# 256-column products of a two-layer hybrid backbone: high and low operand part side by side under one weight load

## The chip, the cores and the metric

The kernel runs on one core of a Trainium2 chip. The metric is device time in microseconds (us) for one execution; the median of 3 runs of the kernel before is 2346.48 us (2346.24 to 2348.11). TensorE is called PE below, its weight loads PEld, VectorE DVE, ScalarE ACT, GpSimd POOL and SyncE SP.

## The reference

Two layers run over 256 context tokens and 256 latent tokens of 1024 channels. Both layers read all 512 tokens, but the last layer needs only the 256 latent tokens as output, so most of its products have 256 token columns.

```python
def hybrid_mixer(h_lat, h_ctx, p, rope_gqa, rope_diff, lam_init, need_ctx):
    ... = jnp.split(h_lat @ p['w_in'], IN_OFFSETS, axis=-1)
    ... = jnp.split(h_ctx @ p['w_in'], IN_OFFSETS, axis=-1)
    ...                       # state-space scan, grouped-query and differential attention
    y_lat = merge_branches(ssm_l, gqa_l, diff_l, gate_l, p)
    if not need_ctx:
        return y_lat, None

def merge_branches(y_ssm, y_gqa, y_diff, gate_logits, p):
    ...
    m = (g[:, :, 0] * (y_ssm @ p['w_ssm_out'])
         + g[:, :, 1] * (y_gqa @ p['w_gqa_out'])
         + g[:, :, 2] * (y_diff @ p['w_diff_out']))
    return m @ p['w_o']

def swiglu(h, w_in, w_out):
    a, b = jnp.split(h @ w_in, 2, axis=-1)
    return (jax.nn.silu(a) * b) @ w_out
```

Every layer then normalises `alpha * x + gate * sublayer(...)` over the channels (layer norm), once after the mixing and once after the feed-forward.

## The kernel before, in words

Activations lie with channels on the 128 partitions and tokens along the free dimension; 1024 channels are `KT` = 8 blocks. A product block is 128 output channels by 512 tokens (layer 0) or 256 tokens (layer 1, `T0` = 256, `TN` = 256), summed over 8 channel blocks in one PSUM tile (`psd`, at most 6 at a time).

To keep float32 accuracy at the rate of the one-pass type float32r, every operand is split into a high part (a rounded copy, made by ACT) and a low part (the difference, made by DVE; `split`, `load_w`). Each product is three matmuls per channel block: high weight times high activation, high weight times low activation, low weight times high activation. `dense` does this for a whole block, `mm3` for one term. In `dense` a pass over the blocks with the high weight comes first, two matmuls each, and then a pass with the low weight. Each matmul has a weight load of its own.

The stages are: layer-0 mixing (projections `proj`, the state-space steps, both attentions, the gated merge), the output product with `w_o` and a layer norm, layer-0 feed-forward, and the same three for layer 1. The 256-column products in layer 0 are the attention's probability-times-value products (`pv_mm`), `w_o`, and the last piece of the feed-forward's output (each done per half of the tokens). In layer 1 nearly all are: 60 projections, 32 branch outputs, `w_o`, 44 feed-forward input blocks and all feed-forward output blocks. Results are read out of PSUM by whoever needs them next: `sigmoid`, the convolution, the rotation, or the residual step `resid`, which adds the gated product to the residual in one DVE instruction.

Nothing is ordered by hand. A class `Plan` records all instructions and then makes a list schedule: it estimates each one's duration (`cost`), keeps track of on-chip tiles (`SIZES`), and fixes the order on every engine; each engine then runs its list in that order, waiting by semaphores. A tile class `s2` has 65 slots of 128 by 512 words that nearly everything shares; in `s2` a slot can hold two tiles of 256 columns. In the trace a tile in such a shared slot is called `shared`, a whole one `s`, a weight tile `w`, a PSUM tile `ps`. All recorded instructions have the line of the one call that emits them, L586 before and L589 after, so the trace is read by tile names and shapes.

## Time and profile before

| what | us |
|---|---|
| median of 3 runs | 2346.48 |
| span of the profiled execution, first to last instruction | 2345.3 |
| PE busy, of the span | 2301.0 (98%) |
| DVE busy | 1670.1 (71%) |
| ACT busy | 1422.4 (61%) |
| layer-0 mixing, 0 to 1007 | 1007 |
| layer-0 output product and norm, 1007 to 1056 | 49 |
| layer-0 feed-forward, 1056 to 1451 | 395 |
| layer-1 mixing, 1451 to 2098 | 647 |
| layer-1 output product and norm, 2098 to 2135 | 37 |
| layer-1 feed-forward, 2135 to 2326 | 191 |
| last layer norm and output, 2326 to the end | 19.3 |

Only one execution was profiled. Its time outside the span isn't listed; the median of the runs lies 1.2 us above the span. The stage borders are read from the order of the weights in the trace, to a microsecond or so. A busy PE is one whose matmuls overlap without a gap, which says nothing of how far apart they start; for that, a stretch's length is divided by its number of matmuls.

### The profile page before, as it was taken

The page shows a single profiled execution, that of the slowest core. Times are in us where ns is not written, and L with a number is a line of the kernel's source. Part 1 is how long each engine was busy: PE and PEld are TensorE (multiplying, and loading weights), DVE is VectorE, ACT ScalarE, POOL GpSimd, SP SyncE. Part 2 cuts the span into 40 slices and gives each one's busy share as a digit, 9 for nine tenths or more (in the row PEclk, how much of TensorE's full clock was granted, in tenths as well). Part 3 has the DMA queues.
Part 4 walks back from the last instruction along what each step waited for, and adds up shares of the span by engine and source line. Part 5 has one row for each costly group of instructions (what it writes and reads, how often), then busy time and mean ns, then how long its engine had stood idle before and what let it go on. Part 6 is the DMA issues. An engine that isn't in the chain of part 4 may idle for free. (4 is left out here: it accounts for less than half of the span.)

```text
span 2345.3 us, 38903 instructions
## 1 busy us (share of the span) xinstructions
PE 2301.0 (98%) x14423; PEld 1940.3 (83%) x14423; DVE 1670.1 (71%) x3438; ACT 1422.4 (61%) x2887; POOL 135.1 (6%) x216
## 2 busy tenths in 40 slices
PE   8999999999999999999999999999999999999998
PEld 4877777887887788898777778989988798998997
DVE  3889857888988864476333337999698888767655
ACT  4778745867767753345323235888586676646554
POOL 3102102000100100000000000001010100000000
PEclk9999999999999999999999999999999999999998
DMA  9746544332433465576555425527443345798662
GB/s 332 214 135 175 181 132 135 102 112 72 133 104 98 133 216 175 184 219 213 171 163 168 139 74 151 150 76 217 132 129 114 105 126 164 214 274 240 191 188 66
DMA packets 520702, 370.37 MB, mean 158 GB/s; under 512 B 20706, under 2 KB 472674, under 8 KB 520512
## 3 DMA queue, kind: packets, MB, share of 16 engines
q1 hardware_dynamic: 507296, 329.63, 47.3%
q0 software_dynamic: 13216, 38.25, 5.5%
q8 instruction: 113, 1.85, 0.3%
q14 instruction: 77, 0.63, 0.1%
HBM read 334.00 MB, written 33.82 MB: 157 GB/s over the span
## 5 line engine op out<-in xcount | busy, mean ns | idle before, releaser
L586 PE MATMUL ps<-s,w 128*128 128x512 f32 (+2 forms) x7608 | 1524.0, 355 | 8.2 <-DVE s L586 4.6
L586 PEld LDWEIGHTS ps<-s,w 128*128 128x128 f32 (+1 forms) x7608 | 1236.0, 189 | 237.1 <-issue 28.8
L586 ACT CAST w<-w 128x1024 fp32r<-128x1024 f32 (+2 forms) x486 | 454.4, 944 | 486.3 <-DVE w L586 256.8
L586 DVE TENSOR_TENSOR w<-w,w 128x1024 fp32r<-128x1024 f32 (+2 forms) x486 | 528.0, 1092 | 299.8 <-PE ps L586 203.0
L586 PE MATMUL ps<-shared,w 128*128 128x256 f32 x2544 | 313.2, 283 | 0.0
L586 PE MATMUL ps<-s,s 128*64 128x128 f32 (+6 forms) x2320 | 303.2, 361 | 7.6 <-DVE s L586 2.1
L586 PEld LDWEIGHTS ps<-shared,w 128*128 128x128 f32 x2544 | 308.5, 192 | 0.5 <-issue 0.3
L586 ACT ACTIVATE s<-s 128x512 f32<-128x512 f32 x424 | 260.6, 630 | 31.0 <-DVE s L586 24.7
L586 PEld LDWEIGHTS ps<-s,s 128*64 128x64 f32 (+3 forms) x2320 | 186.9, 152 | 90.6 <-issue 31.9
L586 DVE TENSOR_TENSOR s<-s,s 128x512 f32<-128x512 f32 (+2 forms) x298 | 196.2, 674 | 36.7 <-ACT s L586 34.5
L586 DVE TENSOR_TENSOR s<-s,ps 128x512 f32<-128x512 f32 x116 | 79.1, 684 | 133.3 <-PE ps L586 65.7
L586 DVE SCALAR_TENSOR_TENSOR s<-ps,misc,s 128x510 f32<-128x510 f32 (+2 forms) x188 | 139.3, 741 | 13.9 <-ACT s L586 11.8
L586 PE MATMUL ps<-w,s 128*128 128x256 f32 x960 | 119.7, 284 | 0.0
L586 PEld LDWEIGHTS ps<-w,s 128*128 128x128 f32 x960 | 117.2, 192 | 2.2 <-issue 1.5
L586 DVE TENSOR_TENSOR shared<-shared,shared 128x256 f32<-128x256 f32 (+2 forms) x241 | 97.2, 417 | 24.4 <-ACT shared L586 22.6
L586 DVE TENSOR_TENSOR s<-ps,s 128x256 fp32r<-128x256 f32 (+1 forms) x204 | 85.6, 444 | 30.4 <-ACT s L586 25.7
L586 ACT ACTIVATE shared<-shared 128x256 f32<-128x256 f32 x232 | 92.4, 416 | 23.4 <-DVE shared L586 20.7
L586 ACT CAST s<-ps 128x256 fp32r<-128x256 f32 (+1 forms) x204 | 74.4, 396 | 36.0 <-PE ps L586 32.1
L586 ACT ACTIVATE s<-ps,misc 128x512 f32<-128x512 f32 x68 | 50.6, 744 | 73.2 <-PE ps L586 73.0
L586 POOL DMA_DIRECT2D s<-dram x96 | 71.9, 753 | 375.0 <-PE ps L586 274.7
L586 ACT ACTIVATE s<-ps,tiny 128x512 f32<-128x512 f32 x112 | 76.7, 689 | 26.5 <-DVE tiny L586 18.9
L586 DVE SCALAR_TENSOR_TENSOR shared<-ps,misc,shared 128x256 f32<-128x256 f32 (+2 forms) x144 | 67.2, 478 | 29.4 <-PE ps L586 20.4
(102 smaller groups left out, 1512.5 us busy)
## 6 DMA issues: line engine op xcount, KB each, us to landing
w<-in_w_in_dram SPq DMA_DIRECT2D x200, 512.0 KB, 4.0
s<-in_ada_w_dram SPq DMA_DIRECT2D x192, 256.0 KB, 4.9
w<-in_ffn_w_in_dram SPq DMA_DIRECT2D x88, 512.0 KB, 3.9
s<-dram POOLq DMA_DIRECT2D x96, 256.0 KB, 5.6
s<-dram SPq DMA_DIRECT2D x64, 256.0 KB, 4.1
w<-in_w_ssm_out_dram SPq DMA_DIRECT2D x32, 512.0 KB, 4.1
w<-in_ffn_w_out_dram SPq DMA_DIRECT2D x32, 512.0 KB, 3.9
shared<-dram SPq DMA_DIRECT2D x112, 128.0 KB, 3.9
```

What stands on the lines that cost most here:

```text
L586: getattr(attr[op.eng], fn)(*[real(v) for v in args], **{a: real(v) for a, v in kw.items()})
```

## The change

For an operand of 256 columns, high and low part are now kept beside each other in one tile of 128 x 2 x 256 (`operand`; for the layer's input streams a new tile class `x4`, 8 tiles of 128 x 2 x 512, `stream`). `side_by_side` then does one matmul of 512 columns with the high weight, which fills a whole PSUM bank (high product in columns 0 to 255, low product in 256 to 511), and one of 256 columns with the low weight, added to the first half. So there are two matmuls for each term where there were three; the columns that stream through are as many as before.

The two halves of the bank must be added. `summed` does it by an ACT copy of the second half into a new tile and a DVE addition of the first half; what read PSUM before now reads that tile. For the residual steps, `resid_halves` does `resid` twice, once for each half. In the attentions, the transposed probabilities of both query halves now go into one PSUM tile per 256 keys (`to_keys`), so the transposes wait for both.

By the loops in the code, 1712 terms are changed: 96 in layer-0 attention, 128 in layer-0 `w_o`, 96 in the last piece of layer-0 feed-forward output, 800 in layer-1 mixing (480 in 60 projections, 256 in 32 branch outputs, 64 in attention), 64 in layer-1 `w_o`, 528 in layer-1 feed-forward (352 in, 176 out). 184 products get `summed` (32 in layer-0 attention, 108 in layer-1 mixing, 44 in layer-1 feed-forward); 24 grouped-query outputs lose an ACT copy that they had before. 64 residual steps become two (16 and 8 after `w_o`, 16 and 24 in the feed-forward).

Three things come with it. `s2` has 49 slots instead of 65, since `x4` takes the room of 16. The planner's cost of a float32r matmul is changed to columns / 2.4 plus weight columns / 9.6 ns. And `HALVES`, the number of first projections of a layer that are done in two halves of 256 columns the old way, now counts only projections over all 512 tokens, so three projections of layer 1 that were done with 512-column matmuls are done in halves: 72 matmuls more. As the planner orders everything anew, hardly a row of any engine stays where it was.

```diff
-SIZES = {"cst": 1, "id": 1, "w4": 15, "s2": 65, "misc": 4, "tiny": 40, "ps": 8}
+SIZES = {"cst": 1, "id": 1, "w4": 15, "x4": 8, "s2": 49, "misc": 4, "tiny": 40, "ps": 8}
...
             if rhs.dt() == F32R:
-                return max(n / 2.4 if n >= 256 else 4 * n / 2.4, 107) + 2.5
+                return (n if n >= 256 else 4 * n) / 2.4 + m / 9.6
...
+    def operand(n):
+
+        if n == 256:
+            t = plan.tile("s2", [128, 2, 256], F32R)
+            return t[:, 0, :], t[:, 1, :], t
+        return t2(n, F32R), t2(n, F32R), None
+
+    def side_by_side(ps, terms):
+
+        both = ps.rearrange("p (a b) -> p a b", b=256)
+        for k, (wh, _, x) in enumerate(terms):
+            T.matmul(both, wh, x[2], start=k == 0, stop=False)
+        for k, (_, wl, x) in enumerate(terms):
+            T.matmul(ps[:, 0:256], wl, x[0], start=False, stop=k == len(terms) - 1)
+
+    def summed(ps):
+        s = t1()
+        A.copy(s, ps[:, 256:512])
+        V.tensor_tensor(s, s, ps[:, 0:256], ALU.add)
+        return s
...
+    def product(w, kn, xs, n):
+        if n == 256:
+            return summed(halves_of(w, kn, xs))
+        ps = psd()
+        dense(ps[:, 0:n], w, kn, xs)
+        return ps
...
+    def stream(x0):
+
+        t = plan.tile("x4", [128, 2, NT], F32R)
+        return t[:, 0, x0:], t[:, 1, x0:], t[:, :, NT - 256:]
...
             w = load_w(W[:, col:col + cols], KT, cols, step)
+            if a:
+                return product(w, KT, xcols(a, NT), NT - a)
             ps = psd()
             half[0] -= 1
-            if half[0] >= 0 and a == 0:
+            if half[0] >= 0:
...
+        def resid_halves(o, d, ps, prev, gm, r):
+            resid(o, d, ps[:, 256:512], prev, gm, r)
+            resid(o, d, ps[:, 0:256], o, gm, r)
...
-                ps = psd()
-                dense(ps[:, 0:256], w, KT, lambda k: tuple(a[:, t0 - T0:t0 - T0 + 256] for a in mm[k]))
-                resid(rt[d, t0], d, ps[:, 0:256], xa, 2, r)
+                resid_halves(rt[d, t0], d, halves_of(w, KT, lambda k: mm[k][t0]), xa, 2, r)
...
+                if not need_ctx:
+                    pab.append(product(w, KT, lambda k: hT[k], TN))
+                    continue
...
-            passes = [[s] for s in segs] if j1 == 22 else [segs]
+            passes = [[s] for s in segs] if j1 == 22 or not need_ctx else [segs]
```

On PE, in the last piece of layer 1's feed-forward output: `ps_24723` is the sum of the second channel block in the order before, `shared_...` its activation tiles (high and low of one block share a tile, hence x2), `w_4687` its high weight and `w_4688` its low weight.

```order
L586 MATMUL ps_24723<-shared_28_24647,w_4687_24565 128x256 x2
L586 MATMUL ps_24723<-shared_3_24717,w_4687_24565 128x256 x2
L586 MATMUL ps_24723<-shared_28_24361,w_4688_24598 128x256
L586 MATMUL ps_24723<-shared_39_24438,w_4688_24598 128x256
L586 MATMUL ps_24723<-shared_30_24505,w_4688_24598 128x256
```

The same place of the change, `ps_23598` being the sum of the fourth channel block:

```order
L589 MATMUL ps_23598<-s_4719_23494,w_4745_23501 128x512
L589 MATMUL ps_23598<-s_4731_23567,w_4745_23501 128x512
L589 MATMUL ps_23598<-s_4671_23260,w_4746_23526 128x256
L589 MATMUL ps_23598<-s_4683_23318,w_4746_23526 128x256
L589 MATMUL ps_23598<-s_4695_23377,w_4746_23526 128x256
```

Where two matmuls of 256 columns stood for the high weight, one of 512 stands now; those for the low weight are as they were.

On DVE, at the end of layer-1 mixing, the branch outputs before: `ps` tiles are products, the `w` rows make low weights of 128 x 1024.

```order
L586 TENSOR_TENSOR shared_56_21458<-shared_56_21458,ps_21931 128x256
L586 TENSOR_TENSOR shared_56_21458<-shared_56_21458 128x256
L586 TENSOR_TENSOR shared_46_20488<-shared_56_21458,shared_36_19583 128x256
L586 TENSOR_TENSOR shared_25_21358<-shared_25_21358,ps_21964 128x256
L586 TENSOR_TENSOR w_4221_22008<-w_4219_21819,w_4220_21968 128x1024
```

And in the change:

```order
L589 TENSOR_TENSOR shared_53_20701<-shared_53_20701,ps_21231 128x256
L589 TENSOR_TENSOR shared_36_20542<-shared_36_20542,shared_53_20701 128x256
L589 TENSOR_TENSOR shared_36_20542<-shared_36_20542 128x256
L589 TENSOR_TENSOR w_4265_21283<-w_4263_21176,w_4264_21269 128x1024
L589 TENSOR_TENSOR s_4222_21280<-shared_36_20542,s_4222_21280 128x256
```

The row that multiplied the gate straight with the PSUM tile has become two: one adds the halves, the next multiplies the sum.

On DVE at the program's end, the last two channel blocks' residual steps before, each followed by the addition that collects the layer norm's sum (`shared_16_21337`), and the first step of the norm itself (it reads `ps_24883`):

```order
L586 SCALAR_TENSOR_TENSOR shared_50_22480<-ps_24839,misc_12157,shared_50_22480 128x256
L586 TENSOR_TENSOR shared_16_21337<-shared_16_21337,shared_50_22480 128x256
L586 SCALAR_TENSOR_TENSOR shared_50_22480<-ps_24860,misc_12157,shared_50_22480 128x256
L586 TENSOR_TENSOR shared_16_21337<-shared_16_21337,shared_50_22480 128x256
L586 SCALAR_TENSOR_TENSOR shared_49_23274<-ps_24883,shared_49_23274 128x256
```

And in the change:

```order
L589 SCALAR_TENSOR_TENSOR shared_53_20701<-ps_23650,misc_11982,shared_53_20701 128x256 x2
L589 TENSOR_TENSOR shared_67_22361<-shared_67_22361,shared_53_20701 128x256
L589 SCALAR_TENSOR_TENSOR shared_38_22415<-ps_23666,misc_11982,shared_38_22415 128x256 x2
L589 TENSOR_TENSOR shared_67_22361<-shared_67_22361,shared_38_22415 128x256
L589 SCALAR_TENSOR_TENSOR shared_16_10462<-ps_23685,shared_16_10462 128x256
```

The residual step stands twice (x2) in front of each addition.

## Rows read from the trace of the kernel before

**Rows 1.** The page's first part: span, then busy us (share) xinstructions by engine

```profile
span 2345.3 us, 38903 instructions
PE 2301.0 (98%) x14423; PEld 1940.3 (83%) x14423; DVE 1670.1 (71%) x3438; ACT 1422.4 (61%) x2887; POOL 135.1 (6%) x216
```

**Rows 2.** Windows by stage: start:end length, busy us (xinstructions) by engine, granted clock, DMA

```profile
core 0: us, PE busy (x) PEld busy (x) DVE busy (x) ACT busy (x) POOL busy (x), PEclk, DMA share, GB/s
0.00:1007.00 1007.00, 988.66 (x5504) 782.33 (x5505) 745.63 (x1677) 647.68 (x1387) 92.90 (x151) 0.99 0.52 156
1451.00:2098.00 647.00, 637.73 (x4595) 572.61 (x4594) 549.60 (x1158) 475.98 (x1034) 42.22 (x65) 0.99 0.54 156
2098.00:2135.00 37.00, 31.73 (x246) 25.86 (x244) 23.47 (x46) 14.58 (x26) 0.00 (x0) 0.95 0.79 229
2135.00:2326.00 191.00, 190.77 (x1588) 190.57 (x1588) 122.48 (x185) 102.22 (x167) 0.00 (x0) 1.00 0.58 169
2326.00:2345.30 19.30, 8.07 (x36) 3.93 (x36) 7.74 (x20) 9.10 (x21) 0.00 (x0) 0.68 0.15 55
```

**Rows 3.** Windows: a 512-column stretch, two crowded DVE stretches, a 256-column stretch

```profile
870.00:986.00 116.00, 116.00 (x513) 96.05 (x512) 49.83 (x57) 46.73 (x59) 1.08 (x2) 1.00 0.61 190
1508.00:1566.00 58.00, 58.00 (x357) 50.74 (x357) 55.92 (x129) 52.43 (x125) 2.20 (x4) 1.00 0.34 99
1566.00:1624.00 58.00, 58.00 (x470) 52.19 (x470) 54.97 (x134) 50.06 (x125) 8.16 (x12) 1.00 0.54 152
2146.00:2320.00 174.00, 174.00 (x1453) 174.00 (x1452) 109.83 (x158) 94.30 (x150) 0.00 (x0) 1.00 0.63 182
```

**Rows 4.** PE groups by shape in 870 to 986: xcount | busy us, mean ns | idle before

```profile
L586 PE MATMUL ps<-s,w 128*128 128x512 f32 x513 | 116.4, 389 | 0.0
```

**Rows 5.** PE groups by shape in 2146 to 2320

```profile
L586 PE MATMUL ps<-shared,w 128*128 128x256 f32 x1453 | 174.5, 283 | 0.0
```

**Rows 6.** DVE and ACT groups by shape over the whole span, nearest to the evictions

```profile
L586 DVE SCALAR_TENSOR_TENSOR shared<-ps,misc,shared 128x256 f32<-128x256 f32 x128 | 59.6, 479 | 29.3 <-PE ps L586 20.4 <-ACT shared L586 6.4 <-DMA shared<-dram 2.3
L586 DVE TENSOR_TENSOR shared<-shared,ps 128x256 f32<-128x256 f32 x92 | 38.1, 416 | 14.4 <-PE ps L586 10.1 <-DMA shared<-dram 2.1 <-ACT shared L586 0.5
L586 ACT COPY shared<-ps 128x256 f32<-128x256 f32 x32 | 11.9, 371 | 13.0 <-PE ps L586 9.9 <-issue 1.7 <-DVE shared L586 1.3
```

**Rows 7.** Timeline of the end: start us, us, engine, xcount, [idle before, releaser]

```profile
2325.94 0.48 DVE L586 SCALAR_TENSOR_TENSOR shared<-ps,misc,shared 128x256 f32<-128x256 f32 x1 [1.21 <-PE ps L586]
2326.46 0.42 DVE L586 TENSOR_TENSOR shared<-shared,shared 128x256 f32<-128x256 f32 x1
2326.94 0.70 PE L586 MATMUL ps<-shared,cst 128*128 128x256 f32 x2 [1.03 <-DVE shared L586]
2327.68 2.74 DVE L586 SCALAR_TENSOR_TENSOR shared<-ps,shared 128x256 f32<-128x256 f32 x8 [0.79 <-PE ps L586]
```

**Rows 8.** DVE's waits in 1451 to 2098: us in total, times, longest us

```profile
DVE w L586 <- PE ps L586: 39.2, 44, 3.2
DVE s L586 <- ACT s L586: 20.1, 31, 2.1
DVE shared L586 <- ACT shared L586: 16.6, 26, 3.0
```

**Rows 9.** PE's waits in 1451 to 2098

```profile
PE ps L586 <- ACT s L586: 4.4, 5, 2.8
PE ps L586 <- DVE s L586: 3.5, 4, 2.3
```

More of the change, by code (lines that the diff above doesn't have):

```diff
@@ L283, in record @@
             b = v.buf
-            group = b.sums.get(v.box) if eng == "PE" and not kw.get("start", True) else None
+            group, box = None, v.box
+            if eng == "PE" and not kw.get("start", True):
+                box, group = next((x, g) for x, g in reversed(b.sums.items()) if _covers(x, v.box))
             if group:
@@ L292, in record @@
                 if eng == "PE":
-                    b.sums[v.box] = [k]
-            b.writes = [w for w in b.writes if not _covers(v.box, w[0])] + [(v.box, k)]
-            b.reads = [w for w in b.reads if not _covers(v.box, w[0])]
+                    b.sums.pop(box, None)
+                    b.sums[box] = [k]
+            b.writes = [w for w in b.writes if not _covers(box, w[0])] + [(box, k)]
+            b.reads = [w for w in b.reads if not _covers(box, w[0])]
         if eng == "PE":
@@ L900, in trunk @@
     make_ada(0, (0, 2), "aw0")
-    xT += [(t2(NT, F32R), t2(NT, F32R)) for _ in range(KT)]
+    xT += [stream(0) for _ in range(KT)]
     load_x(0)
@@ L1391, in trunk @@
             V.tensor_tensor(o, o, t, ALU.add)
-            mh, ml = t2(TN, F32R), t2(TN, F32R)
-            split(mh, ml, o)
-            mm.append((mh, ml))
+            mm.append({})
+            for t0, _ in segs:
+                mm[d][t0] = operand(256)
+                split(mm[d][t0][0], mm[d][t0][1], o[:, t0 - T0:t0 - T0 + 256])
         def layer_norm(rt, t0):
@@ L1445, in norm_stage @@
             xd = dram([KT, 128, NT])
-            xn = [(t2(NT - x0, F32R), t2(NT - x0, F32R)) for _ in range(KT)]
+            xn = [stream(x0) for _ in range(KT)]
             rss = []
@@ L1506, in trunk @@
                 V.tensor_tensor(sg, sg, pab[1], ALU.mult)
-                hh, hl = t2(TN, F32R), t2(TN, F32R)
-                split(hh, hl, sg)
-                hid.append((hh, hl))
+                if j1 < 22 and need_ctx:
+                    hid.append(operand(TN))
+                    split(hid[-1][0], hid[-1][1], sg)
+                else:
+                    hid.append({})
+                    for t0, _ in segs:
+                        hid[-1][t0] = operand(256)
+                        split(hid[-1][t0][0], hid[-1][t0][1], sg[:, t0 - T0:t0 - T0 + 256])
                 next(adas, None)
```

90 lines of the change are left out of this document (47 added, 43 removed).

## The prediction

> **What bounds the kernel now.** The page's first part says that PE is busy for 2301.0 of 2345.3 us [rows 1]. That alone doesn't say that PE runs at its peak, so I looked next at the windows by stage [rows 2] and then at two stretches in which PE does nothing else than one shape of matmul, for the distance between matmuls. In 870 to 986 all 513 are 512 columns wide [rows 4], PE is busy for the whole 116.00 us at a granted clock of 1.00 [rows 3], and they stand 116 / 513 = 226.1 ns apart. In 2146 to 2320 all 1453 are 256 columns wide [rows 5], PE is busy for the whole 174.00 us at the same clock [rows 3], and they stand 174 / 1453 = 119.8 ns apart. The mean durations in those rows (389 and 283 ns) are of overlapping matmuls and are not what one costs. From the pair of distances: 256 more columns cost 106.3 ns, which leaves 226.1 - 2 x 106.3 = 13.5 ns per matmul that doesn't depend on its columns. That is what this change is about: the columns stay, the matmuls become fewer.
>
> Next I looked at who could take PE's place. In layer-1 mixing DVE is busy for 549.60 of 647 us (85%) and ACT for 475.98 (74%) [rows 2]; in 1508 to 1624 DVE is at 55.92 and 54.97 of 58 us, and PE there still hasn't a gap [rows 3]. Of DVE's idle time in that stage 39.2 us are waits of weight splits for PE to let go of a weight buffer [rows 8], so DVE is ahead of PE there and not behind. PE's own waits of the stage are small, 4.4 and 3.5 us in their two largest kinds [rows 9]. So PE's rate of matmuls bounds nearly all of the kernel; its exceptions are the layer norms, where the chain runs through DVE and ACT: in 2098 to 2135 PE is busy for 31.73 of 37 us, and after 2326 for 8.07 of 19.3 [rows 2].
>
> **The matmuls.** A term of 256 columns costs 3 x 119.8 = 359.4 ns now and 226.1 + 119.8 = 345.9 ns after: 13.5 ns less. 1712 terms: 23.1 us. The three layer-1 projections that are now done in halves add 72 matmuls without adding columns, 72 x 13.5 ns = 1.0 us. PE's net gain is 22.1 us, on the engine that bounds; by stages it is 1.3 (layer-0 attention), 1.7 and 1.3 (the rest of layer 0), 9.8 in layer-1 mixing (800 terms less the 1.0), 0.9 and 7.1 (`w_o` and feed-forward of layer 1).
>
> One thing of this isn't in the trace: for the 832 terms of layer-1 projections and feed-forward input, the wide matmul reads two runs of 256 columns that lie 512 apart in an `x4` tile; all 512-column matmuls of rows 4 read one run. I bound its cost between nothing and the 13.5 ns that a matmul of its own would cost, so 0 to 11.2 us, and take nothing, as the row that it's nearest to is the wide matmul's; the upper end stays in the range. A gain is excluded, since as many columns have to pass.
>
> The Trainium skill's page "TensorE: Matmul & The Clock Gate", section "Back-to-back issue gap", gives for warm back-to-back matmuls columns / 2.4 + 2.5 ns. By it a matmul less is worth 2.5 ns and the whole PE term (1712 - 72) x 2.5 ns = 4.1 us instead of 22.1. The trace doesn't agree with it in these streams, where each matmul has a weight load of its own: 226.1 and 119.8 ns are 12.8 and 13.1 above columns / 2.4.
>
> **The evictions.** 184 products get an ACT copy of 371 ns and a DVE addition of 416 ns [rows 6]; back to back, a DVE operation of this size takes less, 2.74 us for eight, so 343 ns [rows 7]. 24 ACT copies go. 64 residual steps are done twice, 479 ns for the second one [rows 6]. In layer-1 feed-forward that is 44 additions and 24 residual steps, some 30 us at most on a DVE that is busy for 122.48 of 191 us [rows 2]; the cover is the other products' matmuls, with up to six sums in PSUM, and nothing is left to pay. In layer-0 mixing 32 additions go to a DVE at 745.63 of 1007 us: nothing either. With that cover gone each product would cost PE the chain of copy and addition, 0.8 us.
>
> Layer-1 mixing is the place where it may cost. DVE gets 108 additions, 37 us (at 343 ns) to 45 us (at 416 ns), ACT 108 copies less 8, 37 us. DVE would then be at about 549.6 + 41 = 591 of 637 us, 93% on the average of the stage. The price lies between nothing, as in the crowded stretches of rows 3 (95.6% over both) where PE waits for nothing, and the whole 45 us, were every addition to lie between PE and its next sum. It's nearer to the crowded stretches, which are the same kind of work at the same fill; I take 4 us, one tenth of the added work, since the average of 93% means some stretches at 100%. A gain here has no source: no DVE or ACT work goes except those copies.
>
> **The chains at the ends.** Where PE has nothing else to do, the second residual step lengthens the chain by one DVE operation, 0.34 to 0.48 us. This is so in the last norm, where the step of 0.48 us starts when PE is done (2325.94) [rows 7]; I count as much for the norm after `w_o` in layer 1, and twice for the last piece of layer-0 feed-forward. Four times 0.48: 2 us. The transposes in the attentions now wait for both query halves; there the scheduler has other work for PE, and the bounds are those of layer-1 mixing.
>
> **Sum.** 2345.3 - 22.1 + 4 + 2 = 2329.2 us of span. The median of the runs is 1.2 us above the span of the profiled execution, so 2330.4; I say 2330.
>
> **Rivals.**
> The wide matmul over two parts is served as two and keeps the second 13.5 ns. For the 832 terms with runs apart the time is 2330.4 + 11.2 = 2341.6; for all 1712 it is 2330.4 + 23.1 = 2353.5. Against it: in the 512-column stretch the fixed part is there once, not twice [rows 3]. For it: no row has a two-part operand. 7%.
>
> The 13.5 ns belongs to something that doesn't go with the matmul, a weight load that is only half covered, say, and that the neighbours then pay. The gain is then less than 22.1 us, with nothing left of it 2330.4 + 22.1 = 2352.5. Against it: wide and narrow matmuls show the same 13.5 ns although the wide one leaves its weight load twice the time. 3%. The page's 2.5 ns would be of this kind, 22.1 - 4.1 = 18.0 us later than the forecast, 2348, no change; the distances of rows 3 don't agree with it.
>
> DVE's list takes over in layer-1 mixing, and the kernel becomes slower. The mechanism: a sum's bank is free only when its addition has run, the addition stands in DVE's list behind weight splits and the state-space work, and with six banks full PE waits. The gain after the end chains is 22.1 - 2 = 20.1 us, so over 108 products this decides from 0.19 us a product onwards (2346.5); at 0.23 us it is 2351, and at 0.38 us (all 41 us) 2367. For it: 55.92 of 58 us before anything is added. Against it: DVE's 39.2 us of waiting for PE's weight buffers [rows 8]. 12%.
>
> The new order is better than the old one. Every engine's list is made anew, with durations for the two matmul shapes that come nearer to 226.1 and 119.8 ns than the former ones did. PE's idle time is 2345.3 - 2301.0 = 44.3 us [rows 1]; were a third of it to go, with nothing lost in layer-1 mixing, the time would be 2330.4 - 15 - 4 = 2311, at a quarter of that 2325. Below 2320: 13%. The opposite, that 16 slots fewer in `s2` cost as much, is in the upper part of the forecast's own range.
>
> That the change doesn't do what it says is excluded by the built order: in layer 1's feed-forward the 512-column rows stand where pairs did.
>
> **How the numbers follow.** Forecast 65%, 2320 to 2341. The two cases of a matmul that isn't cheaper, 10% together, 2341 to 2353. DVE takes over 12%, 2345 to 2367. A better order 13%, 2311 to 2320. A difference under 0.2%, 4.7 us, is about what can't be told from no change; so faster means below 2341.8, slower above 2351.2. Faster: 65 + 13 and a fifth of those 10, 0.80. Same: most of those 10 and a third of DVE's 12, 0.11. Slower: 0.09. The range for 8 in 10 leaves the outer parts of the last three cases out: 2316 to 2346.
>
> **What would show it.** PE's count falls from 14423 [rows 1] to 14423 - 1712 + 72 = 12783, DVE's rises by 184 + 64 and some splits. In layer 1's feed-forward a matmul mix of half 512, half 256 columns should stand (226.1 + 119.8) / 2 = 173 ns apart; 180 ns would show the two-part operand costing as two. That stage should take 191 - 7 = 184 us, layer-1 mixing 637 + 4 = 641. If layer-1 mixing takes longer than 655 and PE's waits there name DVE, DVE has taken over; if the stage is below 635, the order is better.

## The result, and the profile after

The changed kernel takes 2367.59 us (median; 2366.49 to 2369.52), the kernel before 2346.36 us in the same comparison: ratio 1.0091, 95% interval 1.0076 to 1.0105. It is slower by 21 us, where 16 us less were forecast, and the time lies outside the predicted range. The first part of its page, and its windows by stage (columns as in [rows 2], the borders again the stage borders):

```profile
span 2367.4 us, 36232 instructions
PE 2298.4 (97%) x12783; PEld 1854.6 (78%) x12783; DVE 1755.7 (74%) x3700; ACT 1468.7 (62%) x3061; POOL 134.8 (6%) x216
```

```profile
0.00:1034.00 1034.00, 995.91 (x5408) 780.16 (x5409) 757.47 (x1717) 650.05 (x1409) 92.77 (x151) 0.99 0.51 152
1034.00:1082.00 48.00, 48.00 (x282) 40.98 (x281) 43.28 (x82) 25.02 (x38) 0.00 (x0) 1.00 0.74 222
1082.00:1475.00 393.00, 393.00 (x1950) 311.23 (x1951) 187.09 (x306) 150.18 (x227) 0.00 (x0) 1.00 0.50 154
1475.00:2123.00 648.00, 634.04 (x3869) 530.61 (x3868) 587.80 (x1275) 501.96 (x1131) 42.00 (x65) 1.00 0.55 155
2123.00:2163.00 40.00, 33.13 (x190) 24.68 (x188) 26.82 (x56) 17.34 (x30) 0.00 (x0) 0.91 0.72 211
2163.00:2349.00 186.00, 185.73 (x1055) 163.19 (x1056) 144.99 (x248) 115.11 (x208) 0.00 (x0) 0.99 0.60 173
2349.00:2367.40 18.40, 8.57 (x39) 3.80 (x38) 8.29 (x21) 9.10 (x21) 0.00 (x0) 0.82 0.16 58
```

PE's count is exactly the 12783 that was forecast. Beside the stages before and the prediction's sum for each (its terms by stage, taken from the length before):

| stage | before | forecast | after | missed by |
|---|---|---|---|---|
| layer-0 mixing | 1007 | 1005.7 | 1034 | 28.3 |
| layer-0 `w_o`, norm | 49 | 47.3 | 48 | 0.7 |
| layer-0 feed-forward | 395 | 394.7 | 393 | -1.7 |
| layer-1 mixing | 647 | 641.2 | 648 | 6.8 |
| layer-1 `w_o`, norm | 37 | 36.6 | 40 | 3.4 |
| layer-1 feed-forward | 191 | 183.9 | 186 | 2.1 |
| last norm, output | 19.3 | 19.8 | 18.4 | -1.4 |

Three quarters of the 38.2 us missed lie in layer-0 mixing, where only 96 of the 1712 changed terms are. PE does 96 matmuls fewer there and takes 27 us longer: its idle time grows from 1007 - 988.66 = 18.3 us to 1034 - 995.91 = 38.1 us, and its busy time by 7.2 us. PE's waits in that stage, after (us in total, times, longest):

```profile
PE ps L589 <- ACT s L589: 11.4, 8, 3.8
PE ps L589 <- DVE s L589: 7.8, 12, 2.1
PE ps L589 <- ACT shared L589: 5.7, 6, 1.4
PE ps L589 <- DVE x L589: 4.6, 1, 4.6
```

The same view of the kernel before:

```profile
PE ps L586 <- DVE s L586: 6.4, 5, 2.9
PE ps L586 <- ACT shared L586: 2.8, 5, 0.8
PE ps L586 <- ACT s L586: 2.5, 3, 1.2
```

No single wait explains the loss. PE's waits for operands that ACT and DVE make in chains (a rounded copy, then a difference, then a matmul) went from 13 waits of 11.7 us together to 27 of 29.5 us. Yet ACT and DVE do nearly the same work there as before (650.05 and 757.47 us; 647.68 and 745.63 in [rows 2]). This points to the order and not to the load; the runs below test it.

Part of PE's longer busy time is its clock. In the middle of the stage the granted clock fell twice to half (1.2 instead of 2.4 GHz), which it did not in the kernel before. Just ahead of it PE had been busy for only 3.46 of 4.60 and 6.16 of 10.50 us. The changed kernel:

```profile
670.00:674.60 4.60, 3.46 (x26) 2.43 (x27) 4.60 (x14) 4.24 (x12) 0.00 (x0) 1.00 0.48 138
675.00:678.00 3.00, 3.00 (x9) 2.30 (x8) 3.00 (x13) 1.56 (x4) 0.00 (x0) 0.50 0.00 0
756.00:766.50 10.50, 6.16 (x44) 4.28 (x42) 9.29 (x28) 5.36 (x15) 0.00 (x0) 1.00 0.42 124
767.00:773.00 6.00, 5.16 (x18) 4.11 (x19) 5.03 (x16) 4.69 (x14) 0.00 (x0) 0.50 0.00 0
```

The kernel before:

```profile
50.00:1007.00 957.00, 949.38 (x5334) 763.55 (x5333) 728.82 (x1612) 625.83 (x1345) 74.66 (x113) 1.00 0.49 147
```

Over the whole stage PE was busy for 15.7 us at the half clock in the changed kernel and for 9.0 us before (what isn't in the rows above lies in the first 64 us). By the start times of single records, matmuls of 512 columns stand 427 ns apart there instead of 227, so some 3 of the 7.2 us are the clock; this is an estimate from these four numbers.

### The profile page after: what moved, and what is told of

It reads as the page before. It is cut to its first block, busy times and chain, and to the rows that moved or that the text cites. A ratio compares the mean times of both kernels' runs of the same rounds, so it can differ in the third digit from the quotient of the medians.

```text
span 2367.4 us, 36232 instructions
## 1 busy us (share of the span) xinstructions
PE 2298.4 (97%) x12783; PEld 1854.6 (78%) x12783; DVE 1755.7 (74%) x3700; ACT 1468.7 (62%) x3061; POOL 134.8 (6%) x216
## 3 DMA queue, kind: packets, MB, share of 16 engines
q8 instruction: 101, 1.65, 0.3%
## 4 chain that ended last, share of the span: by engine, by line
PE 49%; issue 31%; ACT 8%; DVE 6%; DMA 2%; POOL 0%; POOLq 0%; SPq 0%; ACTq 0%; DVEq 0%
PE ps L589 49%; ACT s L589 4%; ACT shared L589 3%; DVE s L589 3%; DMA s<-dram 1%; DVE shared L589 1%; DVE w L589 1%; ACT w L589 1%; DVE tiny L589 1%; DMA dram<-shared 1%; DMA shared<-dram 0%; POOL s L589 0%; DMA w<-in_w_in_dram 0%; DMA dram<-s 0%; POOL dram L589 0%
## 5 line engine op out<-in xcount | busy, mean ns | idle before, releaser
L589 PE MATMUL ps<-x,w 128*128 128x512 f32 (+3 forms) x6080 | 1290.8, 366 | 9.9 <-DVE x L589 6.7
L589 PEld LDWEIGHTS ps<-x,w 128*128 128x128 f32 (+1 forms) x6080 | 1024.9, 189 | 219.4 <-issue 26.5
L589 PE MATMUL ps<-s,w 128*128 128x512 f32 (+1 forms) x2592 | 532.1, 362 | 0.7 <-DVE s L589 0.7
L589 PEld LDWEIGHTS ps<-s,w 128*128 128x128 f32 x2592 | 439.1, 189 | 84.7 <-issue 7.0
L589 ACT COPY shared<-ps 128x256 f32<-128x256 f32 (+2 forms) x292 | 107.0, 369 | 73.9 <-PE ps L589 59.1
L589 ACT ACTIVATE shared<-shared 128x256 f32<-128x256 f32 x302 | 120.6, 416 | 37.6 <-DVE shared L589 32.3
L589 PE MATMUL ps<-w,x 128*128 128x256 f32 x960 | 122.4, 287 | 0.0
L589 PEld LDWEIGHTS ps<-w,x 128*128 128x128 f32 x960 | 118.9, 194 | 3.4 <-issue 2.0
L589 DVE SCALAR_TENSOR_TENSOR shared<-ps,misc,shared 128x256 f32<-128x256 f32 x160 | 72.4, 480 | 16.1 <-PE ps L589 13.0
L589 DVE TENSOR_REDUCE tiny<-ps 128x1 f32<-128x512 f32 (+1 forms) x144 | 81.1, 592 | 2.6 <-PE ps L589 2.5
```

The source lines that it names most:

```text
L589: getattr(attr[op.eng], fn)(*[real(v) for v in args], **{a: real(v) for a, v in kw.items()})
```

## The experiments: which part costs it

Each is the kernel before or the changed kernel with the edits named; each was compared with the kernel before on the same chip (medians 2347 to 2348 us), and ratios come with their 95% interval. "More" and "slower" are against that kernel. First, what comes along with the change was put alone into the kernel before, or taken out of the change.

**The planner's duration alone, in the kernel before.** It is nearer to what the trace shows: 226.7 and 120.0 ns by the new formula, where rows 3 gave 226.1 and 119.8 ns; the old one says 215.8 and 109.5 ns.

```diff
-                return max(n / 2.4 if n >= 256 else 4 * n / 2.4, 107) + 2.5
+                return (n if n >= 256 else 4 * n) / 2.4 + m / 9.6
```

> The kernel before with the new duration of a float32r matmul in the planner's table, and nothing else. The matmuls are the same 14423; only the order changes. Theory P (the new durations upset the order, among other things how the side branches are mixed into the state-space steps): layer-0 mixing lengthens from 1007 to 1025 us or more, the time is 2362 to 2375. Theory M (the room taken by x4) and theory T (the attention's new form): no change, 2341 to 2351, or a little faster since the durations are nearer to the measured ones.

```profile
0.00:1036.00 1036.00, 1002.40 (x5506) 788.25 (x5507) 747.24 (x1678) 645.03 (x1387) 92.81 (x151) 0.99 0.51 152
1478.00:2148.00 670.00, 646.62 (x4616) 575.84 (x4615) 556.32 (x1168) 478.91 (x1036) 41.90 (x65) 0.99 0.54 151
```

Measured 2388.3 us, 1.0174 (1.0158 to 1.0190): 41 us more, though no engine gets another instruction. This is theory P, with a loss 13 us above its range: layer-0 mixing takes 29 us longer and layer-1 mixing 23.

**The reverse: the change with the old duration** (the same diff on the changed kernel, + and - exchanged).

> The changed kernel with the former duration of a float32r matmul in the planner's table. Theory P: the loss in layer-0 mixing goes and the gain in the feed-forward stays, 2330 to 2345. Theories M and T: as slow as the change, 2360 to 2372.

Measured 2358.33 us, 1.0047 (1.0030 to 1.0064): 9 us of the loss go, and layer-0 mixing is at about 1018 us, so something else costs there too. The time lies between the two ranges.

**The new attention alone, in the kernel before**: `operand`, `side_by_side`, `summed` and the new `to_keys` for the attentions' products only.

```diff
-        def to_keys(p, pt, nk, half):
+        def to_keys(p, nk):
...
-                        to_keys(p2[0], pt, nk, half)
+                        probs.append(p2[0])
...
-                    ps = pv_mm(v, hd % 2, pt, nk)
+                    ps = pv_mm(v, hd % 2, to_keys(probs, nk))
```

> The kernel before with the new attention alone (both query halves transposed into one bank, two matmuls a term, halves added on eviction), in both layers. 160 terms, so PE saves 2.2 us. Theory T (transposes that wait for both halves, probabilities that live longer, a longer chain per head): layer-0 mixing is 1020 us or more, the time 2358 to 2370. Theories P and M: 2340 to 2350.

Measured 2358.44 us, 1.0048 (1.0031 to 1.0065): 11 us slower, where its 160 terms should have given 160 x 13.5 ns = 2.2 us. Layer-0 mixing is at about 1018 us.

**Only the later transposes**, with the attention's old matmuls and without `summed`: both query halves' transposes after both halves' probabilities.

```diff
-                        to_keys(p2[0], pt, nk, half)
+                        probs.append(p2[0])
...
+                    for half in range(2):
+                        to_keys(probs[half], pt, nk, half)
```

> The kernel before with the attention's transposes of both query halves recorded after the second half's probabilities, as in the change; matmuls, splits and evictions as before. If the lateness is what costs in b_attn, 2353 to 2362 with layer-0 mixing at 1015 or more. If it is the new form of the product (copy and addition in the chain, other tiles), no change, 2341 to 2352.

```profile
0.00:1013.00 1013.00, 991.83 (x5505) 782.11 (x5506) 746.04 (x1677) 646.25 (x1387) 92.45 (x151) 0.99 0.52 155
2104.00:2145.00 41.00, 32.53 (x246) 25.61 (x244) 23.12 (x45) 14.64 (x25) 0.00 (x0) 0.88 0.73 210
```

Measured 2359.25 us, 1.0051 (1.0036 to 1.0066): 11 us more, as with the whole new attention. But the two lose it in different places. Here layer-0 mixing grows by 6 us (1013, where 1015 or more was expected) and layer 1's `w_o` stage by 4; with the whole new attention layer-0 mixing grows by 11. So the later transposes are enough for a loss of this size; that the matmul form and the eviction have no part in the other one is not shown.

**The memory alone**: `x4`, and 49 slots of `s2`.

```diff
-SIZES = {"cst": 1, "id": 1, "w4": 15, "s2": 65, "misc": 4, "tiny": 40, "ps": 8}
+SIZES = {"cst": 1, "id": 1, "w4": 15, "x4": 8, "s2": 49, "misc": 4, "tiny": 40, "ps": 8}
```

> The kernel before with the input streams in the class x4 and s2 cut from 65 to 49 slots, and nothing else. Theory M (16 slots that nobody else can use when the streams aren't alive, above all in the first 100 us, where the modulation weights want them): the first stretches are several us slower and layer-0 mixing is 1020 us or more, the time 2358 to 2370. Theories P and T: no change, 2341 to 2351.

Measured 2347.23 us, 1.0000 (0.9991 to 1.0009): nothing.

**The evictions alone**: in the kernel before, 92 layer-1 mixing products get an ACT operation and a DVE addition in the place where the change has them (the first writes zeros, so that the sums stay the same).

```diff
+    def summed(ps):
+        s = t1()
+        A.activation(s, ps[:, 0:256], AF.Identity, scale=0.0)
+        V.tensor_tensor(s, s, ps[:, 0:256], ALU.add)
+        return s
...
-            return ps
+            return summed(ps) if a else ps
```

> The kernel before with the change's eviction work alone, on the 60 projections and 32 branch outputs of layer 1: an ACT instruction on 256 columns from PSUM (scaled by zero) and a DVE addition of the 256-column product to it, whose result is what readers take; the three matmuls a term stay. Theory E (evictions fill DVE and ACT in layer-1 mixing and eat the matmuls' gain there): that stage goes from 647 to 655 or more, the time to 2354 to 2366. If they are covered, as the forecast had it but for 4 us, 2344 to 2352.

```profile
PE 2299.6 (98%) x14423; PEld 1938.5 (83%) x14423; DVE 1699.4 (72%) x3530; ACT 1450.4 (62%) x2979; POOL 134.8 (6%) x216
```

```profile
1450.00:2097.00 647.00, 637.02 (x4593) 570.29 (x4593) 576.60 (x1245) 501.28 (x1122) 42.15 (x65) 1.00 0.55 154
2097.00:2140.00 43.00, 34.22 (x249) 27.54 (x247) 26.51 (x50) 17.04 (x28) 0.00 (x0) 0.88 0.77 217
```

Measured 2352.4 us, 1.0020 (1.0010 to 1.0031), 5 us more. The page shows what was added: DVE 3530 - 3438 = 92 and ACT 92 operations, 29.3 us of DVE and 28.0 us of ACT [rows 1]. The stage in which they stand, layer-1 mixing, takes 647 us as before: the evictions are covered there. The 5 us are in the next one, `w_o` with its norm (43 us instead of 37), which takes 41 us with the later transposes too, without one added operation; so they can't be called the evictions' price.

**The change with the old duration and the old attention**, which leaves the matmul form of projections, branch outputs, `w_o` and feed-forward, the evictions and `x4`.

> The changed kernel with the former matmul duration in the planner and the former attention (three matmuls a term there, 160 terms fewer of the new form). If the two losses found so far (41 us of the durations and 11 us of the attention, each alone on the kernel before) are what covers the gain, PE's saving shows: 1552 terms of 13.5 ns less 1.0 us, 20 us, so 2326 to 2336. If evictions or memory cost as much too, 2341 or more.

Measured 2348.91 us, 1.0005 (0.9996 to 1.0014), where 2326 to 2336 was expected. Duration and attention together carry 18.7 of the 21 us. Its windows of layer-0 mixing, layer-1 `w_o` and layer-1 feed-forward:

```profile
0.00:1006.00 1006.00, 986.99 (x5506) 781.16 (x5507) 747.70 (x1685) 647.60 (x1394) 92.64 (x151) 1.00 0.53 156
2096.00:2141.00 45.00, 33.99 (x190) 22.99 (x188) 30.65 (x65) 19.59 (x34) 0.00 (x0) 0.88 0.74 215
2141.00:2327.00 186.00, 185.78 (x1053) 163.12 (x1054) 145.20 (x248) 115.12 (x208) 0.00 (x0) 0.99 0.59 173
```

Layer-0 mixing is back at its old length. But a kernel with 1480 matmuls fewer than before (1552 terms, less the 72) is only as fast as before: layer-1 feed-forward gains 5 us, layer-1 mixing only 1 (646 us), and in the `w_o` stage, where 33.99 us of PE's work take 45 us, 8 us are lost.

**That, with projections and branch outputs of layer 1 old as well**, so that only `w_o` and the feed-forward keep the new form.

```diff
-            if a:
-                return product(w, KT, xcols(a, NT), NT - a)
...
-                ps = product(w, KT, lambda k: y[k], TN)
+                ps = psd()
+                dense(ps[:, 0:TN], w, KT, lambda k: y[k])
```

> a_oldboth with the 60 projections and 32 branch outputs of layer-1 mixing in the former form too, so that the new form is left in w_o (192 terms), the feed-forward of layer 1 (528) and the last piece of layer 0's (96): 816 terms of 13.5 ns are 11 us at most; the wide matmuls of the feed-forward were seen 231 and not 226 ns apart, which leaves 7 to 8. Theory E: 2336 to 2344, faster than both kernels, with layer-1 mixing at 647. If the planner's order is what decides, anywhere from 2340 to 2360.

Measured 2354.74 us, 1.0029 (1.0017 to 1.0042): slower still, with less changed. Its layer-0 mixing is the work of the kernel before, without one changed term, and takes about 1014 us instead of 1006. That is the order again, and no changed matmul.

## The experiments: why better durations make a worse order

The planner uses the duration in two places: in the list schedule, and when the program is recorded, where `RATIO` of the matmul time spent decides how much of a side branch is dealt out between the main products. They were parted.

**New duration in the dealing out only**, schedule as before:

```diff
-            self.spent["PE"] += dur
+            n = self.free(ins[1]) if fn == "matmul" else 0
+            self.spent["PE"] += (n if n >= 256 else 4 * n) / 2.4 + ins[0].shape[-1] / 9.6 if n and ins[1].dt() == F32R else dur
```

> The kernel before; the new matmul duration is used only where the side branches (attentions and merges) are dealt out against the state-space steps, by PE work brought so far; the schedule itself keeps the old durations. Theory P1 (the dealing out is upset): most of the 41 us of b_cost are here, 2370 to 2390, layer-0 mixing 1025 or more. Theory P2 (the schedule is upset by the durations themselves): no change, 2341 to 2353.

Measured 2367.18 us, 1.0083 (1.0068 to 1.0098), 19 us more; layer-0 mixing takes about 1029 us.

**New duration in the schedule only** (the edit of the first experiment, and the old formula kept for `self.spent`):

> The counterpart of b_spent: the new matmul duration only in the schedule (start times, priorities), the dealing out of the side branches by the old one. P1: no change, 2341 to 2353. P2: 2370 to 2390.

Measured 2380.67 us, 1.0138 (1.0121 to 1.0155), 33 us more, and here the program recorded is that of the kernel before, instruction for instruction. So both uses cost, each alone; their sum, 52 us, is more than the 41 of both together. Its windows of the two mixing stages, and PE's waits in the first:

```profile
0.00:1034.00 1034.00, 999.83 (x5506) 785.40 (x5507) 749.45 (x1678) 647.13 (x1387) 92.48 (x151) 0.99 0.51 152
1477.00:2134.00 657.00, 644.58 (x4608) 573.34 (x4607) 554.11 (x1165) 476.88 (x1034) 42.12 (x65) 1.00 0.54 153
```

```profile
PE ps L587 <- DVE s L587: 10.1, 11, 4.5
PE ps L587 <- ACT s L587: 8.6, 6, 3.8
PE ps L587 <- DVE tiny L587: 6.3, 6, 1.6
```

This is the picture of the changed kernel: layer-0 mixing at 1034 us, and more waits of PE for what ACT and DVE make. From it comes the theory of a **reserve** (R): the list schedule starts a matmul when its operand is ready by the plan. Were the planned matmuls 5 to 9% too short (215.8 for 226.1 ns, 109.5 for 119.8 ns), then PE on the chip reached each consumer later than planned, and the chain through ACT and DVE had that much spare time. With the right length the plan has no spare time left, and each delay of ACT, DVE or a semaphore that the plan has too short makes PE wait. If so, the same right durations with longer planned delays should be good again.

**Right durations, and 150 ns more on the delays between engines** (three of the four numbers are delays; `HOP` enters the priorities):

```diff
-FREE, TO_PE, TICK = 250, 270, 10240 / 3
-HOP, SLACK, SPARE = 300, 10000, 1
+FREE, TO_PE, TICK = 250, 420, 10240 / 3
+HOP, SLACK, SPARE = 450, 10000, 1
...
-                        lat = 197
+                        lat = 347
...
-                        lat = 145
+                        lat = 295
```

> b_dur with 150 ns added to every delay that the planner puts between engines; the matmul durations stay the new ones. Theory R (reserve): the former durations, 10 and 5 per cent too short, made the planner put more matmuls between a chain on DVE or ACT and its consumer on PE than the chip needs, and this reserve was lost with true durations; then longer planned delays give it back: layer-0 mixing from 1034 to 1020 or less, the time from 2381 to 2345 to 2362. If the order is only unlucky, it stays at 2372 to 2390.

Measured 2364.04 us, 1.0076 (1.0054 to 1.0098): 17 us above the kernel before instead of 33. Layer-0 mixing is at the 1020 us that theory R asked for, the time 2 us above its range. The two mixing stages, and PE's waits in the first:

```profile
0.00:1020.00 1020.00, 994.17 (x5509) 782.25 (x5510) 746.84 (x1679) 647.03 (x1387) 92.60 (x151) 1.00 0.52 154
1463.00:2111.00 648.00, 635.40 (x4593) 569.94 (x4592) 546.55 (x1155) 474.18 (x1033) 42.18 (x65) 1.00 0.55 155
```

```profile
PE ps L587 <- DVE s L587: 8.8, 13, 2.5
PE ps L587 <- ACT s L587: 4.2, 6, 1.4
PE ps L587 <- DVE tiny L587: 1.5, 2, 0.9
```

**More reserve in the kernel before**: its planned matmuls made 5% shorter still, in the schedule only.

```diff
-                return max(n / 2.4 if n >= 256 else 4 * n / 2.4, 107) + 2.5
+                return 0.95 * (max(n / 2.4 if n >= 256 else 4 * n / 2.4, 107) + 2.5)
```

> The kernel before with the matmul durations of the schedule another 5 per cent shorter, the dealing out of the branches as before. Theory R: the loss goes one way only, so with still more reserve the time is within a few us of the kernel before, 2338 to 2354. If the former durations are a lucky order and any other costs, 2358 to 2385, as in b_dur.

Measured 2357.63 us, 1.0045 (1.0030 to 1.0060), 10 us more: 3.6 us above theory R's range and just below the other one. Both mixing stages keep their lengths (about 1007 and 646 us), as R has it, but the layer-1 `w_o` stage gets 9 us longer, for which R has no reason.

**The same 150 ns in the changed kernel itself** (the diff of the 150 ns above; the right durations are there already).

> The changed kernel itself with 150 ns added to every delay that the planner puts between engines. Theory R (the reserve lost with the true durations): layer-0 mixing from 1034 to 1022 or less, the time from 2368 to 2345 to 2358. Otherwise 2360 to 2375.

```profile
0.00:1013.00 1013.00, 988.03 (x5409) 778.62 (x5410) 753.70 (x1717) 648.96 (x1409) 92.71 (x151) 0.99 0.53 155
1454.00:2098.00 644.00, 632.06 (x3870) 532.85 (x3869) 582.33 (x1270) 500.75 (x1131) 42.26 (x65) 0.99 0.55 155
```

Measured 2349.75 us, 1.0008 (0.9998 to 1.0018). Four numbers of the planner, and 18 of the 21 us are gone; layer-0 mixing is 21 us shorter with the same work as in the changed kernel (5408 matmuls there, 5409 here). Shown is that these four numbers, and nothing else, give back 17 and 18 us in two kernels, mostly in layer-0 mixing, where PE's waits had grown: about half of what the durations cost in the schedule, and most of what the change lost. That this is the reserve is argued and not shown: the run with shorter durations missed theory R's range, the delays and `HOP` were not parted, and the kernel before was not run with longer delays and its own durations. The next run gives a size for what an order by chance can do.

**How much any other order costs.** In the kernel before, only the first ratio was changed, by 1.3%.

```diff
-RATIO = (1.52, 1.42)
+RATIO = (1.50, 1.42)
```

> The kernel before with layer 0's dealing ratio of side branches to state-space steps at 1.50 instead of 1.52, nothing else. Theory S (the constants sit at a point that was chosen for this very program, and any other order costs): 2352 to 2365, all of it in layer-0 mixing. If the order matters little without a change of durations, 2344 to 2350.

```profile
0.00:1015.00 1015.00, 989.08 (x5506) 784.04 (x5507) 748.31 (x1678) 645.19 (x1387) 92.75 (x151) 0.99 0.52 155
```

Measured 2354.85 us, 1.0033 (1.0022 to 1.0044): 7 us, all of them in layer-0 mixing (1015 us instead of 1007), from a number that adds no work. So the kernel before sits at a good point of its own constants, and a difference of some 8 us between two orders needs no other cause. This is one such run, and the size isn't a bound. Eight runs so far order the operations of the kernel before anew without adding one: the memory alone leaves the time as it was, and the other seven are slower, by 7 to 41 us. The 17 us that remain with longer delays, the dealing out's 19 us and the transposes' 11 us are larger than 8, but the runs don't name what in the order does it; the transposes' 11 are not far above it.

## The experiments: what the matmul form is worth

**The change with old duration and old attention, constants set anew** (picked by the length of the planner's own schedule, which is no time of the chip):

```diff
-ROUNDS, GAP, REACH, BUMP = 4, 400, 20000, 1.0
+ROUNDS, GAP, REACH, BUMP = 6, 400, 20000, 1.0
-RATIO = (1.52, 1.42)
+RATIO = (1.66, 1.35)
-HALVES, HALVES_FF = 7, 2
+HALVES, HALVES_FF = 8, 2
```

> a_oldboth (the new matmul form everywhere but in the attentions, short durations) with the dealing ratios at 1.66 and 1.35, eight projections in halves and six planning rounds. Theory S: the gain that the old constants covered shows, 2330 to 2342, faster than both kernels. Theory E (evictions in layer-1 mixing cost what the matmuls save there): that stage stays at 645 or more and the time at 2343 to 2352.

Measured 2344.2 us, 0.9982 (0.9973 to 0.9991): a little faster than the kernel before, with layer-1 mixing at about 646 us. Both are as theory E had them, though by the run above the evictions are covered in that stage; theory S, 2330 to 2342, is missed.

**With only `w_o` and feed-forward in the new form**, and ratios 1.66 and 1.37, 6 rounds:

> a_ff (new form only in w_o, layer-1 feed-forward and the last piece of layer 0's) with ratios 1.66 and 1.37 and six rounds. Theory S: 2338 to 2346, 7 to 8 us of matmuls less than the kernel before and no evictions in layer-1 mixing. Theory E: at least 3 us faster than a_tuned; theory S: slower than a_tuned by some 5 us, since a_tuned has twice the changed terms.

Measured 2352.16 us, 1.0017 (1.0008 to 1.0027), above theory S's range. With the form in layer-1 mixing the kernel is 8 us faster than without it here, and 6 us with the old constants (2348.91 and 2354.74). Theory E expected the opposite, but neither difference is larger than what an order by chance can do.

**Right durations, longer delays, old attention, constants set anew.** The edits of the changed kernel with 150 ns, the old formula for `self.spent`, the attention of before, and:

```diff
-ROUNDS, GAP, REACH, BUMP = 4, 400, 20000, 1.0
+ROUNDS, GAP, REACH, BUMP = 6, 400, 20000, 1.0
-RATIO = (1.52, 1.42)
+RATIO = (1.67, 1.35)
-HALVES, HALVES_FF = 7, 2
+HALVES, HALVES_FF = 6, 2
```

> The changed kernel with the attention of before, the new matmul duration in the schedule but the old formula in the dealing out, 150 ns more on the planner's two delays, and the planner's ratios (1.67 and 1.35), halves (6) and rounds (6) set anew. If the loss of the change was all order, and the new matmul form is worth what its matmuls show one by one, the time is 2332 to 2344 us, under both the kernel before and the earlier version of the change with ratios set anew (2344.2). If the order of the kernel before was merely a good one by chance and each new order costs some us, it is 2346 us or more.

Measured 2341.24 us (2339.26 to 2342.50), 0.9974 (0.9963 to 0.9985), inside the first range.

**The kernel before, constants set anew in the same manner** (ratios 1.65 and 1.37, 8 halves, 6 rounds, gap 500).

> The kernel before with its own matmuls, and only the planner's ratios (1.65 and 1.37), halves (8), rounds (6) and gap (500) set anew. If constants near these are good for any program, 2340 to 2350 us. The comparison that counts is with the changed kernel with constants set anew: if the new matmul form is worth anything by itself, that one is at least 4 us below this one; if the two come out alike, what the constants gave is all that the tuned version of the change gained.

Measured 2352.49 us, 1.0021 (1.0012 to 1.0030): worse than with its own constants, and above the first range. So such constants aren't good for any program; that no others would make the old form as fast is not shown, since this is one set. Mixing stages of both, the new form first, and the new one's `w_o` stage:

```profile
0.00:1009.00 1009.00, 987.42 (x5482) 779.59 (x5483) 746.39 (x1685) 642.30 (x1394) 92.71 (x151) 1.00 0.53 156
1453.00:2093.00 640.00, 629.78 (x3882) 530.74 (x3881) 573.75 (x1246) 498.80 (x1123) 41.93 (x65) 1.00 0.55 156
2093.00:2136.00 43.00, 35.04 (x187) 25.58 (x185) 29.88 (x61) 17.39 (x31) 0.00 (x0) 0.88 0.72 213
```

```profile
0.00:1019.00 1019.00, 994.43 (x5530) 785.70 (x5531) 750.68 (x1678) 644.77 (x1387) 92.98 (x151) 0.99 0.52 154
1460.00:2107.00 647.00, 638.56 (x4639) 573.58 (x4638) 552.63 (x1166) 474.03 (x1033) 41.98 (x65) 1.00 0.55 156
```

Layer-1 mixing takes 640 us in the new form, what the prediction wanted there (641), and 647 in the old one. In the best version found, the new form beats the kernel before by 5.8 us and the old form with constants set anew by 11.2 us; the first is again no more than an order by chance can do. It has 14423 - 12895 = 1528 matmuls fewer (48 of them by the smaller `HALVES`), 21 us at 13.5 ns. By stages it gains 7 us in layer-1 mixing and 5 in layer-1 feed-forward, and loses 6 in layer 1's `w_o` stage (43 us instead of 37) and 2 in layer-0 mixing. One of these gains doesn't hang on the order: layer-1 feed-forward takes 186 us in all six runs with the new form whose stages were read, and 191 to 194 us in those with the old one.

## Why the prediction was wrong, point by point

**What bounds the kernel**: right where PE's streams are dense, and not enough in layer-0 mixing. There the forecast left PE's 18.3 us of idle time [rows 2] as they were. They hang on the order, and can as well be 38 us.

**The matmuls.** Count right (12783). The price holds nearly: layer-1 feed-forward sheds 1588 - 1055 = 533 matmuls and its busy time falls from 190.77 to 185.73 us, 5.0 us, or 9.5 ns a matmul instead of 13.5; after, matmuls stand 185.73 / 1055 = 176 ns apart, where 173 was forecast and 180 would have meant that the two-part operand is served as two. The formula that the prediction took from the page "TensorE: Matmul & The Clock Gate" of the Trainium skill, section "Back-to-back issue gap", is given there for an isolated matmul and not for streams with a weight load for each matmul, as these are. By it 533 x 2.5 ns = 1.3 us would go, an estimate; the trace's 5.0 us doesn't agree with it, and what was measured decides, so the rival built on it falls as well. The prediction's argument that both shapes show the same 13.5 ns is none, since the two distances were solved for just that number. In layer-1 mixing 640 us in the best version match the 641 of the sum, but the other runs with the new form have 644 to 651 us there.

**The two-part operand**: taken as free, and it is, as far as two parts go. Wide matmuls of layer 1's feed-forward stand some 230 ns apart instead of 226, but those whose operand is one run of columns (`s`, 231 ns) do so as well as those of `x4` (230 ns).

**The evictions**: 4 us in layer-1 mixing taken from bounds of 0 and 45; 92 of the 108 alone leave that stage at 647 us. So the term belongs at the lower bound, and that the run as a whole is 5 us longer, close to the 4, is luck: these lie in the `w_o` stage. In the changed kernel PE's largest waits of layer-1 mixing and DVE's for weight buffers are

```profile
PE ps L589 <- DVE s L589: 4.3, 10, 0.9
PE ps L589 <- ACT x L589: 2.8, 1, 2.8
DVE w L589 <- PE ps L589: 19.6, 19, 4.8
```

so DVE's spare time before weight splits is halved (39.2 us in [rows 8]), and it hardly holds PE up: all of PE's waits that name DVE add up to 7.3 us in that stage, and to 3.7 before. The rival in which DVE's list takes over would have shown the stage above 655 us with DVE in PE's waits: it is at 648. Its range reached 2367, but the mechanism isn't what happened.

**The chains at the ends**: the second residual step is there, 1.00 us for the pair where one took 0.48 [rows 7], here the last one before the norm:

```profile
2349.39 1.00 DVE L589 SCALAR_TENSOR_TENSOR shared<-ps,misc,shared 128x256 f32<-128x256 f32 x2 [0.63 <-PE ps L589]
2350.43 0.42 DVE L589 TENSOR_TENSOR shared<-shared,shared 128x256 f32<-128x256 f32 x1
```

The size is right for the step, and the last stage, 18.4 us instead of 19.3, got no longer. Layer 1's `w_o` stage grew by 3 us, though, and varied from about 33 to 46 us over the runs, 46 in one (planned matmuls 5% shorter) without any residual step doubled.

**The step that failed** is the last one, "The new order is better than the old one". The prediction saw that every engine's list is made anew "with durations for the two matmul shapes that come nearer to 226.1 and 119.8 ns than the former ones did", and counted that as a gain or nothing. The only loss that it allowed for was that of 16 slots fewer in `s2`, within the forecast's own range; that one measured nothing. In layer-0 mixing it priced only 96 terms, at 1.3 us. The nearer durations alone cost 41 us in the old program, and without them the changed kernel is 9 us faster. The second half of the failure is in "The chains at the ends": the transposes that wait for both query halves were given the bounds of the evictions, on the ground that PE has other work there, and taken as nothing; alone they go with a loss of 11 us in the old program. The two losses don't simply add up, since the change as a whole is only 21 us slower, but without both it is at 2348.91 us, with layer-0 mixing back from 1034 to 1006 us.

From 2348.91 to the forecast of 2330 another 19 us are missing. By the stages of that run, beside the forecast's, about 8 of them lie in layer 1's `w_o` stage, 5 in layer-1 mixing (646 instead of 641), 2 in layer-1 feed-forward and the rest in smaller pieces. The first two change with the planner's constants alone (38 to 45 us and 640 to 646 us over the three versions with the old attention), so they are at least partly order too.

**What stays open**: whether the reserve is what longer delays give back; what the dealing out's 19 us hang on; the 17 us that remain with right durations and longer delays; and the part of PE's longer busy time in layer-0 mixing (7.2 us after, 11.2 us with the durations alone in the schedule) that isn't the clock, some 4 and 8 us (an estimate as above; with the durations alone PE was busy for 15.3 us at the half clock). It is time between matmuls that the trace doesn't show as waiting.

## What to carry to other kernels

A planner's constants and the order that comes out of them are part of a tuned kernel: a change that also makes a planner's durations truer has to be priced as a change of the whole order before its own saving is counted. Where the constants were chosen for the program as it is, a loss is the likelier outcome: here seven of eight new orders of the same work were slower and none was faster. Make such a change in two steps, first the matmuls with the planner's durations left alone, then the durations together with the planner's delays. And a transposition or copy that waits for two producers instead of one is a lengthened chain, to be priced as such however little it adds in work.

## What was not expected of the hardware

In layer 1's feed-forward of the changed kernel, wide matmuls start about 230 ns after each other (226 to 236, by the start times of the single records), narrow ones still 119.8; in 880 to 996, a layer-0 stretch of nothing but wide ones, it is 116 / 512 = 226.6 ns as before:

```profile
880.00:996.00 116.00, 116.00 (x512) 95.67 (x511) 48.81 (x55) 45.26 (x60) 2.21 (x4) 1.00 0.62 189
```

The granted clock is 0.99 to 1.00 in both. DVE is busier in the slower stretch (144.99 of 186 us against 48.81 of 116), but that isn't the cause. In this stretch of wide matmuls it is busier still, and they start 227.5 ns after each other:

```profile
428.90:441.70 12.80, 12.80 (x58) 10.53 (x58) 12.08 (x31) 12.68 (x31) 0.00 (x0) 1.00 0.45 124
```

The start times show where the nanoseconds go. In the feed-forward wide and narrow matmuls mostly come in runs of eight. The first five wide ones after a run of narrow ones stand 233, 236, 229, 232 and 231 ns before the next, the last three 227 as elsewhere; the best version shows the same to a nanosecond. So a change from narrow to wide costs about 27 ns, and the first narrow one after wide ones, at 114 ns, gives 6 back: some 1.4 us over the stage's 528 / 8 = 66 changes, two thirds of the 2.1 us missed there. Why the change costs anything is open.

At the half clock the part that doesn't depend on the columns is not to be seen: in 60.5 to 63.5 of the changed kernel narrow matmuls stand 213 ns apart and in 675 to 677 wide ones 427, twice as much. So the 13.5 ns were seen at the full clock only.
